# Convolution taps and softmax sums moved from VectorE to GpSimd, SSD decays moved out of attention

## The chip, the cores and the metric

The kernel runs on one core of a Trainium2 chip. The metric is device time in microseconds for one execution. Five engines work from queues of their own, each strictly in order: TensorE (PE), VectorE (DVE), ScalarE (ACT), GpSimd (POOL) and SyncE (SP), which here issues every DMA.

## The reference

Two layers of a hybrid block over 1024 latent tokens and 256 context tokens, model width 1024, all in float32:

```python
h = modulate(x, norm_g[i], shift, scale); h_c = modulate(ctx, ...)
z, xbc, dtr, q, k, v, ga, ua, ub, gc = split_cols(h @ w_in[i])
# SSD: 5-tap convolution, 12 heads of 64, state 128, chunks of 128, both directions
lmat = exp(where(mask, cum[t] - cum[s], -inf))          # the decays
y_diag = einsum('clsg,clsgr,csgrp->clgrp', C @ B.T, lmat, x * dt)
# attention: 12 heads, 4 key heads, 1280 keys (latents and context)
attn = softmax(q @ k.T) @ v * silu(ga)
# conformer: 31-tap depthwise convolution over 512 channels
u = silu(layernorm(dwconv(ua * sigmoid(ub), cm_conv_w) + cm_conv_b))
conv = (u @ pw_w + pw_b) * silu(gc)
x = x + gate * (concat([ssd, attn, conv]) @ w_out[i])
```

After the second layer a last rmsnorm gives the output. In layer 1 the context's rows are needed as keys and as the SSD's initial state alone, so there the conformer runs over 1024 columns and not 1295.

## The kernel before, in words

A product in float32 is made of three products of rounded halves (hi x hi, hi x lo, lo x hi; `mm3`). Weights are split as they arrive: ScalarE rounds the upper half (`wth`), GpSimd subtracts (`wtl`, L359).

Each layer goes through these stages:

1. Norms, then keys, values and queries in token-major form (`phase_b`).
2. Seventeen blocks of feature-major products (`block(i)`, `FM_UNITS`). Blocks 0 to 8 alternate between pairs of SSD channels (`xbc`) and a pair `ub`, `ua` of the conformer. Blocks 9 to 11 are the gate z, 12 and 13 gc, 14 to 16 ga. A gate goes through tanh on ScalarE and one VectorE instruction to DRAM (`gate`).
3. While these run, the convolutions run on VectorE. `conv_x(j)` is a tensor_scalar, four scalar_tensor_tensor (`xcv`), a tanh and one more, over 1282 columns; PE then transposes the result (`t<-msk,xcv`, `x<-msk,xcv`) and ScalarE copies it to `xsg`, from where it goes to DRAM. `conv_cm(j)`, j from 0 to 3, is one tensor_scalar and 30 scalar_tensor_tensor into the accumulator `cac[j]`. Its input `up` has two buffers, so the third `ua` is written when the first one's 31 taps are done. The tile `th` has one buffer, shared by `conv_x`'s tanh and the gate `ub`.
4. `cm_tail`, with all four `cac` complete: for each tile of 128 tokens PE transposes `cac` (`t<-msk,cac`), VectorE normalises, PE transposes back, silu, the split `uh`, `ul`; for each group of four tiles the pointwise product, times the gate gc. It runs beside blocks 9 to 16.
5. Attention (`attn`) with the SSD (`ssd`) beside it. A unit is two heads by 256 queries: 24 units against 1280 keys a layer, and 6 more of the context in layer 0. `maxima(i)` finds row maxima two units ahead (`a_sm`). `scores(i)` makes ten key tiles of scores and exponentials; these land in pairs, `a_p`, of which there are five buffers. The softmax sums are adds of pairs into `a_ac`, then one add of its halves, `a_a` (L981). `NG = [0, 1]` alternates from unit to unit: all on VectorE, or one add on GpSimd and three on VectorE (an add of two partial sums included). `values(i)` multiplies with v, `finish` sums `a_a` over keys by a product with `twos`, takes the reciprocal, multiplies, gates.
6. The SSD per chunk: `s_cb`, a broadcast load of the cumulated sums; GpSimd subtracts (L788), ScalarE does relu and exp, GpSimd multiplies with the masked B C product `s_cm` (L791); the tile `s_e` is then an operand of PE. Four such tiles a chunk, ten chunks in layer 0, eight in layer 1. Other products of the chunk (`s_wx`, `s_tm`, `s_xd`, `s_yo`) are GpSimd's as well.
7. The output product in two halves (`out_half`).

The order of the work isn't written by hand. `at(us)` gives the following instructions a due time, and when the kernel is built a planner plays the program through with costs of its own and takes, for each engine, the ready instruction with the earliest due time. The order that comes out is fixed; at run time an engine waits for whatever stands first in its queue. A tile pool that opens in the place of a closed one waits for the last user of the closed one's memory.

Of the kernel before, what the change touches and what calls it, by code (L numbers as in the profile page):

```python
# [9 lines left out]
F32R = mybir.dt.float32r  # L10
# [10 lines left out]
CM_PACE = 1.7  # L21
TAIL = 40.0
SSD_PACE = 25.0
# [4 lines left out]
FLAG = 7  # L28
NG = [0, 1]
A2B = 1  # L30
# [8 lines left out]
NT = T // 128  # L39
# [121 lines left out]
def build(tc, a, out, depth=DEPTH, dump=None):  # L161
# [272 lines left out]
    def phase_b(l, nh, b0, pp):  # L434
# [114 lines left out]
        def conv_cm(j, t0, pace):  # L549
            u, o = ups[j], cac[j]  # L550
            at(t0)
            ts(V, o[:, 0:NCM], u[:, 0:NCM], cw[:, j, 0:1], ALU.mult, cc(l, "cmb", j), ALU.add)
            for k in range(1, 31):
                at(t0 + k * pace)
                stt(o[:, 0:NCM], u[:, k:k + NCM], cw[:, j, k:k + 1], o[:, 0:NCM], ALU.mult, ALU.add)

        def conv_x(j, t0):
# [16 lines left out]
            if j < 8:  # L574
                at(t0 + XLAG)
                sg = mk(gp, [128, NT, 128], "xsg")
                for ta in (0, 4, 8):
                    n = min(4, NT - ta)
                    ps = mk(*((pt, [128, 4, 128], "t") if ta == 4 else (px, [128, 4, 128], "x")))
                    for t in range(ta, ta + n):  # L580
                        c0 = t * 128 + (2 if t >= 8 else 0)
                        tr(ps[:, t - ta, :], o[:, c0:c0 + 128], idf)
                    act(sg[:, ta:ta + n, :], ps[:, 0:n, :], AF.Copy)
                if j < 6:
                    d = xt_d[:, :, 128 * j:128 * j + 128]
                else:
                    d = bt_d[:, :, 128 * (j - 6):128 * (j - 6) + 128]
                Y.dma_start(out=d.rearrange("t p f -> p t f"), in_=sg)

# [63 lines left out]
        for i in range(9, 14):  # L653
            block(i)

        def cm_tail(c0):
            at(c0 - 10)
            pwh, pwl = wblock(tlp, wt, a["pww"][l], "pw", 1)
            hc = mk(tlp, [128, 16], "hc")
            ts(V, hc[:, 0:8], colc[l][:, CO["lng"][0]:CO["lng"][0] + 8], 0.5, ALU.mult)  # L660
            groups = [(0, 4), (4, 4)] + ([] if last else [(8, 2)])
            for tb, tn in groups:
                uh = mk(tlp, [128, 4, 512], "uh", F32R)
                ul = mk(tlp, [128, 4, 512], "ul", F32R)
                for t in range(tb, tb + tn):
                    at(c0 + 4 * t)
                    c1 = t * 128 + (15 if t >= 8 else 0)
# [20 lines left out]
                    act(uh[:, :, o:o + 128], v2, AF.Copy)  # L688
                    G.tensor_tensor(ul[:, :, o:o + 128], v2, uh[:, :, o:o + 128].bitcast(F32), ALU.subtract)
# [20 lines left out]
    def ssd(l, sp, c0, sv):  # L710
# [44 lines left out]
        for c in [8, 9] + list(range(8)):  # L755
# [3 lines left out]
            if c < 8 or not last:  # L759
                bT = mk(sp, [128, 2, 128], "s_bT", bufs=2)  # L760
                cT = mk(sp, [128, 2, 128], "s_cT", bufs=2)
                tk = slice(128 * c, 128 * c + 128)
                Y.dma_start(out=bT, in_=bT_d[:, :, tk].rearrange("g p t -> p g t"))
# [3 lines left out]
                ps = mk(px, [128, 512], "x")  # L767
                for g in range(2):
                    mm(ps[:, 128 * g:128 * g + 128], bT[:, g, :], cT[:, g, :], True, True)
                cm = mk(sp, [128, 2, 2, 128], "s_cm", bufs=1)  # L770
                for d, m in enumerate((um, lm)):
                    V.tensor_tensor(cm[:, d], ps[:, 0:256].rearrange("p (g t) -> p g t", g=2),
                                    m.unsqueeze(1).to_broadcast([128, 2, 128]), ALU.mult)
                xd = []
# [5 lines left out]
                for g in range(2):  # L780
                    for d in range(2):
                        h0 = 12 * d + 6 * g
                        cb = mk(sp, [128, 6, 128], "s_cb", bufs=2)
                        src = cum_d[24 * c + h0:24 * c + h0 + 6, :].rearrange("h t -> (h t)")
                        Y.dma_start(out=cb.rearrange("p h t -> p (h t)"),
                                    in_=src.unsqueeze(0).to_broadcast([128, 768]))
                        e = mk(sp, [128, 6, 128], "s_e", bufs=4)
                        G.tensor_tensor(e, cb, bc(cum[:, c, h0:h0 + 6], 6, 128), ALU.subtract)  # L788
                        act(e, e, AF.Relu, scale=-1.0)
                        act(e, e, AF.Exp, scale=-1.0)  # L790
                        G.tensor_tensor(e, e, cm[:, d, g].unsqueeze(1).to_broadcast([128, 6, 128]), ALU.mult)  # L791
                        E[d, g] = e
# [416 lines left out]
```

## Time and profile before

| | |
|---|---|
| median of 3 runs | 2921.86 us (2919.12 to 2928.43) |
| profiled execution | 2926.13 us, span 2924.1 us |
| PE / DVE / ACT / POOL busy | 93% / 74% / 36% / 40% of the span |
| feature blocks, with taps: layer 0, layer 1 | 299.6 to 603.2, 1804.4 to 2068.6 us |
| feature blocks, rest: layer 0, layer 1 | 603.2 to 797, 2068.6 to 2218 us |
| attention with SSD: layer 0, layer 1 | 797 to 1375, 2218 to 2712 us |
| mean granted TensorE clock | 0.965 |

The busy time of an engine counts from an instruction's start to its end, and what an instruction waits for after its start is inside it. PE's busy time is that of pipelined products with modelled ends. A mean over a line mixes instructions that ran alone with others that were held up; the view by tile gives minimum, median and maximum.

### The profile page before, as it was taken

Reading aid. Unit: us, or ns where it says so; the run is one execution under the profiler, and the core shown is the slowest. Engines: PE = TensorE matmul, PEld = TensorE weight load, DVE = VectorE, ACT = ScalarE, POOL = GpSimd, SP = SyncE. Lnnn points to the kernel's source line nnn. Section 1 sums busy time; section 2 is a strip of 40 time slices with the busy share of each in tenths; the row PEclk is TensorE's granted clock in tenths of the full one; section 3 lists DMA queues with packets and bytes.
Section 4 is the critical chain, followed back from the end, with each engine's and each line's share of the span. In section 5 each row is a group of like instructions: output and inputs, shape, how many; then the busy total and the mean of one; then the engine's idle time right before and its main releaser. Section 6 shows DMA issues by size and latency. Waiting matters only on the chain. (4 is left out here: it accounts for less than half of the span.)

```text
span 2924.1 us, 41057 instructions
## 1 busy us (share of the span) xinstructions
PE 2714.5 (93%) x15708; PEld 2111.4 (72%) x15708; DVE 2175.7 (74%) x2987; ACT 1062.2 (36%) x1801; POOL 1165.6 (40%) x832
## 2 busy tenths in 40 slices
PE   5999998999998888999999999999998998999998
PEld 3888876888856655666787998877886665666676
DVE  4476899973299989797445587999835989898644
ACT  4212221222245454454335222222224454644432
POOL 2244122232168677571112352222323667675111
PEclk9999998999999989899999999999999999999999
DMA  6551111223343222224645322113234232312554
GB/s 237 191 159 66 56 55 65 90 98 105 115 137 108 73 88 84 74 68 130 205 147 162 114 76 67 55 63 107 102 127 151 73 98 72 103 59 62 164 152 143
DMA packets 284035, 314.44 MB, mean 108 GB/s; under 512 B 27606, under 2 KB 219190, under 8 KB 282814
## 3 DMA queue, kind: packets, MB, share of 16 engines
q1 hardware_dynamic: 283838, 311.82, 33.5%
q8 instruction: 123, 2.02, 0.3%
q14 instruction: 74, 0.61, 0.1%
HBM read 236.25 MB, written 75.50 MB: 107 GB/s over the span
## 5 line engine op out<-in xcount | busy, mean ns | idle before, releaser
L193 PE MATMUL m<-hh,wth 128*128 128x512 f32 (+1 forms) x1440 | 533.7, 371 | 0.1
L193 PE MATMUL m<-hl,wth 128*128 128x512 f32 (+1 forms) x1440 | 532.2, 370 | 0.0
L193 PE MATMUL m<-hh,wtl 128*128 128x512 f32 (+1 forms) x1440 | 531.6, 369 | 0.0
L199 ACT ACTIVATE a_p<-m 128x512 f32<-128x512 f32 x492 | 285.5, 596 | 373.1 <-PE m L193 362.7
L208 DVE SCALAR_TENSOR_TENSOR cac<-up,cmw,cac 128x1295 f32<-128x1295 f32 (+1 forms) x240 | 383.2, 1617 | 1.9
L935 DVE TENSOR_REDUCE a_sm<-m 128x1 f32<-128x512 f32 (+1 forms) x600 | 331.0, 583 | 52.8 <-PE m L193 50.2
L359 POOL TENSOR_TENSOR wtl<-wr,wth 128x1024 fp32r<-128x1024 f32 x68 | 201.9, 2969 | 404.2 <-ACT wth L199 404.1
L193 PEld LDWEIGHTS m<-hh,wth 128*128 128x128 f32 x1440 | 273.0, 190 | 47.8 <-ACT th L199 0.5
L193 PEld LDWEIGHTS m<-hh,wtl 128*128 128x128 f32 x1440 | 272.5, 189 | 48.1
L193 PEld LDWEIGHTS m<-hl,wth 128*128 128x128 f32 x1440 | 272.7, 189 | 47.3
L193 PE MATMUL m<-q_a,k_a 128*128 128x512 f32 (+1 forms) x656 | 255.3, 399 | 23.1 <-ACT a_p L199 10.9
L193 PE MATMUL m<-k_a,q_a 128*128 128x512 f32 (+1 forms) x600 | 242.0, 440 | 24.9 <-DVE a_sm L935 19.3
L193 PE MATMUL t<-a_p,vs 128*64 128x256 f32 x1968 | 250.9, 397 | 0.9 <-ACT a_p L199 0.4
L193 PE MATMUL m<-woh,yl 128*128 128x512 f32 x576 | 227.7, 397 | 6.1 <-DVE yl L1101 5.9
L193 PE MATMUL m<-woh,yh 128*128 128x512 f32 x576 | 226.6, 396 | 5.2 <-ACT yh L199 5.2
L193 PE MATMUL m<-wol,yh 128*128 128x512 f32 x576 | 226.6, 395 | 0.8 <-DVE wol L1077 0.8
L193 PE MATMUL m<-q_b,k_b 65*128 65x512 f32 (+1 forms) x656 | 223.1, 350 | 0.0
L193 PEld LDWEIGHTS t<-a_p,vs 128*64 128x64 f32 x1968 | 138.7, 142 | 89.1 <-issue 17.2
L193 PEld LDWEIGHTS m<-q_a,k_a 128*128 128x128 f32 x656 | 129.3, 197 | 84.3 <-ACT a_p L199 23.4
L193 PEld LDWEIGHTS m<-k_a,q_a 128*128 128x128 f32 x600 | 117.0, 201 | 99.6 <-DVE a_sm L935 38.2
L199 ACT ACTIVATE wth<-wr 128x1024 fp32r<-128x1024 f32 (+1 forms) x84 | 89.3, 1063 | 255.6 <-DMA wr<-in_wfm 136.2
L193 PE MATMUL m<-wth,hh 128*128 128x256 f32 (+1 forms) x608 | 173.6, 288 | 1.3 <-ACT wth L199 0.8
(239 smaller groups left out, 5629.5 us busy)
## 6 DMA issues: line engine op xcount, KB each, us to landing
wr<-in_wfm SPq DMA_DIRECT2D x68, 512.0 KB, 3.6
s_cb<-cum_d SPq DMA_DIRECT2D x72, 384.0 KB, 3.7
ada_w<-in_adaw SPq DMA_DIRECT2D x32, 512.0 KB, 4.6
wor<-in_wout SPq DMA_DIRECT2D x64, 256.0 KB, 3.1
s_x<-xt_d SPq DMA_DIRECT2D x38, 384.0 KB, 3.2
yf<-ys_d SPq DMA_DIRECT2D x36, 384.0 KB, 3.9
yf<-ya_d SPq DMA_DIRECT2D x36, 384.0 KB, 4.2
yf<-yc_d SPq DMA_DIRECT2D x36, 256.0 KB, 2.9
```

The lines of the kernel that those rows point to most:

```text
L193: P.matmul(o, l, r, start=start, stop=stop)
L199: S.activation(o, i, f, **k)
L208: V.scalar_tensor_tensor(o, i, s, i1, op0, op1)
L359: (e or G).tensor_tensor(lo[:, s], raw, hi[:, s].bitcast(F32), ALU.subtract)
L935: V.tensor_reduce(sm[:, 2 * x + t, j:j + 1], ps[:, 0:kn], axis=AX.X, op=ALU.max)
```

## The change

Three things at once, with the due times that go with them.

- 45 taps a layer leave VectorE: all of `conv_cm(0)` (its first one becomes a ScalarE instruction, 30 become a scaling on ScalarE into `cmt`, of which there are two buffers, and an add on GpSimd) and the last 15 of `conv_cm(2)`.
- The decays are made in a new function `decays`, a chunk in turn with a tile of the conformer tail, and go through DRAM (`e_d`). Their multiplication moves from GpSimd to VectorE. The SSD only loads the finished tiles.
- `NG = [4]`: all four adds of pairs of each unit against 1280 keys are GpSimd's; VectorE keeps `a_a`.

The conformer tail goes in pairs of tiles, due 17 us apart (4 us before), from `TAIL = 20` (40 before). Blocks 9 to 16 get a lead of 100 us in the due times of their weights and of their gates. `xsg` becomes three smaller tiles with a store each.

```diff
-TAIL = 40.0
+TAIL = 20.0
+GTAPS = {0: 30, 2: 15}
-NG = [0, 1]
+NG = [4]
...
         def conv_cm(j, t0, pace):
             u, o = ups[j], cac[j]
             at(t0)
-            ts(V, o[:, 0:NCM], u[:, 0:NCM], cw[:, j, 0:1], ALU.mult, cc(l, "cmb", j), ALU.add)
-            for k in range(1, 31):
+            nv = 31 - GTAPS.get(j, 0)
+            if nv > 1:
+                ts(V, o[:, 0:NCM], u[:, 0:NCM], cw[:, j, 0:1], ALU.mult, cc(l, "cmb", j), ALU.add)
+            else:
+                act(o[:, 0:NCM], u[:, 0:NCM], AF.Identity, scale=cw[:, j, 0:1], bias=cc(l, "cmb", j))
+            for k in range(1, nv):
                 at(t0 + k * pace)
                 stt(o[:, 0:NCM], u[:, k:k + NCM], cw[:, j, k:k + 1], o[:, 0:NCM], ALU.mult, ALU.add)
+            for k in range(nv, 31):
+                at(t0 + (nv - 1) * pace + (k - nv) * 2 * pace)
+                m = mk(up_p, [128, 1295], "cmt", bufs=2)
+                act(m[:, 0:NCM], u[:, k:k + NCM], AF.Copy, scale=cw[:, j, k:k + 1])
+                G.tensor_tensor(o[:, 0:NCM], o[:, 0:NCM], m[:, 0:NCM], ALU.add)
...
         def block(i):
-            at(u0 - 20)
+            lead = 100 if i >= 9 else 0
+            at(u0 - 20 - lead)
...
+                    at(tt - lead)
                     fm_fin(ps, n, j, t0, tn)
...
+        def decays(c, t0):
+            cum = sv[1]
+            at(t0)
+            bT = mk(ep, [128, 2, 128], "e_b")
+            cT = mk(ep, [128, 2, 128], "e_c")
...
+            at(t0 + 8)
+            ps = mk(px, [128, 512], "x")
+            for g in range(2):
+                mm(ps[:, 128 * g:128 * g + 128], bT[:, g, :], cT[:, g, :], True, True)
+            cm = mk(ep, [128, 2, 2, 128], "e_m")
...
+                    at(t0 + 8 + 4 * (2 * d + g))
+                    e = mk(ep, [128, 6, 128], "e_e", bufs=3)
+                    src = cum_d[24 * c + h0:24 * c + h0 + 6, :].rearrange("h t -> (h t)")
+                    Y.dma_start(out=e.rearrange("p h t -> p (h t)"), in_=src.unsqueeze(0).to_broadcast([128, 768]))
+                    G.tensor_tensor(e, e, bc(cum[:, c, h0:h0 + 6], 6, 128), ALU.subtract)
+                    act(e, e, AF.Relu, scale=-1.0)
+                    act(e, e, AF.Exp, scale=-1.0)
+                    V.tensor_tensor(e, e, cm[:, d, g].unsqueeze(1).to_broadcast([128, 6, 128]), ALU.mult)
+                    Y.dma_start(out=e_d[c][2 * d + g], in_=e.rearrange("p h t -> p (h t)"))
...
-            groups = [(0, 4), (4, 4)] + ([] if last else [(8, 2)])
+            groups = [(b, 2) for b in range(0, 8 if last else NT, 2)]
...
-                    at(c0 + 4 * t)
+                    at(c0 + 17 * t)
...
-        cm_tail(g0 + TAIL)
+        order = list(range(8)) if last else [8, 9] + list(range(8))
+        for t in cm_tail(g0 + TAIL):
+            decays(order[t], g0 + TAIL + 17 * t)
...
                 for g in range(2):
                     for d in range(2):
-                        h0 = 12 * d + 6 * g
-                        cb = mk(sp, [128, 6, 128], "s_cb", bufs=2)
...
                         e = mk(sp, [128, 6, 128], "s_e", bufs=4)
-                        G.tensor_tensor(e, cb, bc(cum[:, c, h0:h0 + 6], 6, 128), ALU.subtract)
-                        act(e, e, AF.Relu, scale=-1.0)
-                        act(e, e, AF.Exp, scale=-1.0)
-                        G.tensor_tensor(e, e, cm[:, d, g].unsqueeze(1).to_broadcast([128, 6, 128]), ALU.mult)
+                        Y.dma_start(out=e.rearrange("p h t -> p (h t)"), in_=e_d[c][2 * d + g])
                         E[d, g] = e
```

More of the change, by code (lines that the diff above doesn't have):

```diff
@@ L260, in build @@
     cum_d = dr([NT * 24, 128], "cum_d")
+    e_d = [dr([4, 128, 768], f"e_d{c}") for c in range(NT)]
     gz_d = dr([6, 128, T], "gz_d")
@@ L575, in conv_x @@
                 at(t0 + XLAG)
-                sg = mk(gp, [128, NT, 128], "xsg")
+                if j < 6:
+                    d = xt_d[:, :, 128 * j:128 * j + 128]
+                else:
+                    d = bt_d[:, :, 128 * (j - 6):128 * (j - 6) + 128]
                 for ta in (0, 4, 8):
@@ L582, in conv_x @@
                         tr(ps[:, t - ta, :], o[:, c0:c0 + 128], idf)
[L583 to L588, printed above, removed]
+                    sg = mk(gp, [128, 512], "g_o", bufs=2)[:, 0:128 * n].rearrange("p (t f) -> p t f", t=n)
+                    act(sg, ps[:, 0:n, :], AF.Copy)
+                    Y.dma_start(out=d[ta:ta + n].rearrange("t p f -> p t f"), in_=sg)
         def gate(ps, t0, n, d):
@@ L654, in phase_b, with bc @@
             block(i)
+        def bc(x, n, w):
+            return x.unsqueeze(2).to_broadcast([128, n, w])
+        def decays(c, t0):
+            cum = sv[1]
+            tk = slice(128 * c, 128 * c + 128)
+            at(t0)
+            bT = mk(ep, [128, 2, 128], "e_b")
+            cT = mk(ep, [128, 2, 128], "e_c")
+            Y.dma_start(out=bT, in_=bT_d[:, :, tk].rearrange("g p t -> p g t"))
+            Y.dma_start(out=cT, in_=cT_d[:, :, tk].rearrange("g p t -> p g t"))
+            at(t0 + 8)
[3 more added lines that the diff above has]
+            cm = mk(ep, [128, 2, 2, 128], "e_m")
+            for d, m in enumerate((um, lm)):
+                V.tensor_tensor(cm[:, d], ps[:, 0:256].rearrange("p (g t) -> p g t", g=2),
+                                m.unsqueeze(1).to_broadcast([128, 2, 128]), ALU.mult)
+            for d in range(2):
+                for g in range(2):
+                    h0 = 12 * d + 6 * g
+                    at(t0 + 8 + 4 * (2 * d + g))
[7 more added lines that the diff above has]
+                    Y.dma_start(out=e_d[c][2 * d + g], in_=e.rearrange("p h t -> p (h t)"))
+        ep = pool(s3, f"ep{l}")
         def cm_tail(c0):
@@ L660, in cm_tail @@
             ts(V, hc[:, 0:8], colc[l][:, CO["lng"][0]:CO["lng"][0] + 8], 0.5, ALU.mult)
-            groups = [(0, 4), (4, 4)] + ([] if last else [(8, 2)])
+            groups = [(b, 2) for b in range(0, 8 if last else NT, 2)]
             for tb, tn in groups:
-                uh = mk(tlp, [128, 4, 512], "uh", F32R)
-                ul = mk(tlp, [128, 4, 512], "ul", F32R)
+                uh = mk(tlp, [128, 4, 256], "uh", F32R)
+                ul = mk(tlp, [128, 4, 256], "ul", F32R)
                 for t in range(tb, tb + tn):
-                    at(c0 + 4 * t)
+                    at(c0 + 17 * t)
                     c1 = t * 128 + (15 if t >= 8 else 0)
@@ L674, in cm_tail @@
                     rs_pow(bs[:, 9:10], bs[:, 7:8], 1.0, bs[:, 8:9], 1)
-                    xn = mk(gp, [128, 512], "xn", bufs=1)
+                    xn = mk(tlp, [128, 512], "xn", bufs=1)
                     ts(V, xn, ps.rearrange("p j t -> p (j t)"), bs[:, 6:7], ALU.subtract, bs[:, 9:10], ALU.mult)
@@ L689, in cm_tail @@
                     G.tensor_tensor(ul[:, :, o:o + 128], v2, uh[:, :, o:o + 128].bitcast(F32), ALU.subtract)
+                    yield t
                 n = tn * 128
-                at(c0 + 4 * (tb + tn))
+                at(c0 + 17 * (tb + tn))
                 for f in range(4):
-                    gcs = mk(gp, [128, 512], "gcs")
+                    gcs = mk(tlp, [128, 256], "gcs", bufs=2)
                     Y.dma_start(out=gcs[:, 0:n], in_=gc_d[f][:, tb * 128:tb * 128 + n])
@@ L759, in ssd @@
             if c < 8 or not last:
-                bT = mk(sp, [128, 2, 128], "s_bT", bufs=2)
                 cT = mk(sp, [128, 2, 128], "s_cT", bufs=2)
                 tk = slice(128 * c, 128 * c + 128)
-                Y.dma_start(out=bT, in_=bT_d[:, :, tk].rearrange("g p t -> p g t"))
                 Y.dma_start(out=cT, in_=cT_d[:, :, tk].rearrange("g p t -> p g t"))
@@ L766, in ssd @@
                 Y.dma_start(out=gz, in_=gz_d[:, :, tk].rearrange("g p t -> p g t"))
[L767 to L773, printed above, removed]
                 xd = []
```

3 lines of the change are left out of this document (removed).

## The prediction

> **What bounds the kernel now.** I read the page's slices first, then the table by stage, cut at the first and the last convolution tap of each layer.
>
> ```profile
> DVE  4476899973299989797445587999835989898644
> POOL 2244122232168677571112352222323667675111
> GB/s 237 191 159 66 56 55 65 90 98 105 115 137 108 73 88 84 74 68 130 205 147 162 114 76 67 55 63 107 102 127 151 73 98 72 103 59 62 164 152 143
> ```
> ```profile
> 299.60:603.20 303.60, 278.85 (x1422) 235.24 (x1420) 298.51 (x194) 62.03 (x95) 69.33 (x43) 0.96 0.21 68
> 603.20:797.00 193.80, 193.28 (x1038) 164.90 (x1038) 75.39 (x155) 45.86 (x74) 44.96 (x31) 1.00 0.31 106
> 797.00:1375.00 578.00, 514.96 (x3369) 348.00 (x3370) 504.59 (x707) 295.48 (x509) 370.42 (x222) 0.93 0.31 94
> 1804.40:2068.60 264.20, 251.22 (x1194) 207.07 (x1192) 263.20 (x187) 61.60 (x91) 64.06 (x42) 0.98 0.24 77
> 2068.60:2218.00 149.40, 149.09 (x674) 121.27 (x674) 63.36 (x115) 35.66 (x53) 38.57 (x26) 1.00 0.35 116
> 2218.00:2712.00 494.00, 447.89 (x2922) 302.57 (x2922) 435.04 (x619) 253.42 (x436) 313.18 (x187) 0.95 0.30 90
> ```
>
> The busy columns are PE, PEld, DVE, ACT, POOL; then clock, DMA share, GB/s. Rows 1 and 4 are the taps: DVE is busy 298.5 of 303.6 us and 263.2 of 264.2, POOL a quarter of it. Rows 2 and 5, the rest of the feature products with the conformer tail, are PE alone, never idle. Rows 3 and 6 are attention with the SSD: PE near 90%, DVE 88%, POOL 64%. By these shares POOL is free to relieve DVE. The next rows say why that fails.
>
> ```profile
> 349.71 1.56 DVE L208 SCALAR_TENSOR_TENSOR cac<-up,cmw,cac 128x1295 f32<-128x1295 f32 x1
> 364.71 2.40 POOL L359 TENSOR_TENSOR wtl<-wr,wth 128x1024 fp32r<-128x1024 f32 x1 [14.63 <-ACT wth L199]
> 364.88 3.60 DVE L208 SCALAR_TENSOR_TENSOR cac<-up,cmw,cac 128x1295 f32<-128x1295 f32 x1
> ```
>
> A tap takes 1.56 us alone. The one that starts 0.17 us into a POOL subtraction takes 3.60: it waits until 367.11, when POOL ends, and runs its whole length after that (367.11 + 1.4 = 368.5). A DVE instruction that reads two SBUF operands and a POOL tensor_tensor do not overlap; they take turns. So I keep a ledger: uncontended times of the two kinds, added up, for 299.6 to 603.2.
>
> ```profile
> L208 DVE SCALAR_TENSOR_TENSOR cac<-up,cmw,cac 128x1295 f32<-128x1295 f32 x120 | 209.6, 1765 | 1.0
> L208 DVE SCALAR_TENSOR_TENSOR xcv<-xpad,scw,xcv 128x1282 f32<-128x1282 f32 x32 | 53.1, 1658 | 0.0
> L205 DVE TENSOR_SCALAR xcv<-xpad,scw 128x1282 f32<-128x1282 f32 x8 | 16.0, 1997 | 0.0
> L208 DVE SCALAR_TENSOR_TENSOR xcv<-th,xcv 128x1282 f32<-128x1282 f32 x8 | 11.9, 1485 | 0.0
> L359 POOL TENSOR_TENSOR wtl<-wr,wth 128x1024 fp32r<-128x1024 f32 x19 | 68.0, 3580 | 179.1 <-ACT wth L199 179.1
> ```
> ```profile
> 509.18 0.94 DVE L205 TENSOR_SCALAR cac<-up,cmw,colc 128x1295 f32<-128x1295 f32 x1
> 1979.74 1.27 DVE L208 SCALAR_TENSOR_TENSOR cac<-up,cmw,cac 128x1024 f32<-128x1024 f32 x1
> 1980.94 0.80 DVE L205 TENSOR_SCALAR cac<-up,cmw,colc 128x1024 f32<-128x1024 f32 x1
> ```
>
> Layer 0: 120 x 1.56 + 32 x 1.55 + 12 x 0.94 + 8 x 1.49 + 19 x 2.40 = 305 us in a stretch of 303.6. Layer 1, with taps of 1.27: 152 + 50 + 11 + 12 + 20 x 2.40 = 273 in 264. The taps' stretch is bound by the taking of turns, at 100%, and not by DVE.
>
> How PE pays for it:
>
> ```profile
> PE x L196 <- DVE xcv L208: 12.8, 2, 10.6
> PE x L196 <- ACT xsg L199: 5.4, 2, 5.0
> PE t L196 <- DVE xcv L208: 4.2, 1, 4.2
> PE t L196 <- DVE xcv L208: 11.7, 3, 6.1
> ```
> ```profile
> 505.32 0.42 DVE L208 SCALAR_TENSOR_TENSOR up<-th,m 128x256 f32<-128x256 f32 x1
> 603.23 0.44 PE L196 MATMUL t<-msk,cac 128*128 128x128 f32 x2 [2.44 <-DVE cac L208]
> 1979.15 0.68 DVE L208 SCALAR_TENSOR_TENSOR up<-th,m 128x512 f32<-128x512 f32 x1
> 2068.68 0.44 PE L196 MATMUL t<-msk,cac 128*128 128x128 f32 x2 [1.26 <-DVE cac L208]
> ```
>
> The first three rows are layer 0's, the fourth layer 1's (total us, times, longest). PE's queue has one order, laid down in advance; transposes of the convolved tiles stand between feature products, and PE waits for them: 24.8 us in layer 0 (12.8 + 5.4 + 4.2 + 2.4), 13.0 in layer 1. DVE's own excess is 298.5 minus its uncontended 273 (260 for two operands, 13 for 22 PSUM ones of 0.42 to 0.68), about 25. I conclude that the order was planned as if the two engines did not hinder each other.
>
> **The change, part by part.**
>
> *45 taps a layer.* Each leaves DVE (1.56 us, layer 1 1.27) and becomes a scaling on ScalarE and an add on POOL. Its price in turns is bounded by the plain adds:
>
> ```profile
> L974 POOL TENSOR_TENSOR a_ac<-a_p,a_p x24: 2358/2373/3350, 844.8 to 2720.8; 128x1024 f32<-128x1024 f32 x24
> L689 POOL TENSOR_TENSOR ul<-lv,uh x18: 1282/1294/1337, 617.1 to 2156.9; 128x512 fp32r<-128x512 f32 x18
> L199 ACT ACTIVATE th<-xcv x20: 1262/1276/1285, 267.3 to 2036.3; 128x1282 f32<-128x1282 f32 x20
> ```
>
> (2.37 - 1.29)/512 = 2.11 ns a column, so 2.37 + 271 x 2.11 ns = 2.94 us for 1295 columns; 2.37 for layer 1's 1024. The ledger grows by 45 x (2.94 - 1.56) = 62 us in layer 0 and 45 x (2.37 - 1.27) = 49 in layer 1. Bounds: minus 70 and minus 57 if POOL's adds cost DVE nothing (the 3.60 row excludes most of that), plus 62 and 49 if all collide. Since the ledger is full, I take the upper ends. ScalarE's 46 instructions of 1.28 us (59 us a layer) fit: it is busy 62 of 303.6. POOL in order has the weight splits (wtl) between the adds; PE stands a block of weights ahead, so I cost that at nothing; if the lead is lost, each block waits for one or two adds, 3 to 9 us.
>
> The Trainium skill, "SBUF — State Buffer", section "Who interferes with whom", states the mechanism as a rule: a VectorE instruction with two SBUF inputs and a GpSimd one that reads SBUF share a port pair under an exclusive lock held for the whole instruction. The 3.60 us row agrees with it. By the rule the taps cost 62 and 49 us; by the busy shares alone they would save 70 and 57. "GPSIMD Engine Reference" of the Trainium skill, "Performance versus the Vector engine", gives 4497 ns for an add of 2048 columns, in proportion 2.84 us for 1295: by it the sum would be 58 instead of 62.
>
> So the last tap of layer 0 ends near 603 + 62, less two or three weight splits that PE's wait holds back (6): 660. In layer 1: 2069 + 49 - 5 = 2113.
>
> *Where PE meets it.* In the planned order DVE has fewer taps, so the tail's first transposes stand earlier. After the last gated piece (505.7 us, less the 22.4 that PE had waited by then: 483) DVE has block 3's 31 taps (47.7), two SSD convolutions (17.2) and a few gates (3.5): 551 on a clock without waits, where before it was 603.2 - 24.8 = 578. The new due time (TAIL 20, then 17 us a tile) is earlier still, so it doesn't hold them back. PE arrives early and waits until 660: 109 us lost in place of 24.8, a loss of 84. Part of it falls sooner: the third `up` buffer is the first one again, free only when block 0's 30 adds are done (88 us of adds with 8 to 10 splits and DVE's turns after 300, so 445 to 475, where PE wants it at 411). The ledger's end is the same. Layer 1: 1979.8 - 11.7 + 39 + 17.2 + 2.7 = 2027, waits until 2113: 86 in place of 13.0, a loss of 73.
>
> *Decays.* Per chunk 4 subtractions, 8 activations, 4 multiplications (now on DVE), 2 mask products, 2 products, and 10 DMAs (bT and cT, 4 loads, 4 stores) go beside blocks 10 to 16; in the SSD 4 loads stay, of the finished tiles.
>
> ```profile
> L788 POOL TENSOR_TENSOR s_e<-s_cb,d_cum x72: 1462/1472/2537, 810.0 to 2648.3; 128x768 f32<-128x768 f32 x72
> L791 POOL TENSOR_TENSOR s_e<-s_e,s_cm x72: 1806/1856/2824, 878.2 to 2665.6; 128x768 f32<-128x768 f32 x72
> L199 ACT ACTIVATE s_e<-s_e x144: 827/843/851, 811.5 to 2650.7; 128x768 f32<-128x768 f32 x144
> L974 DVE TENSOR_TENSOR a_ac<-a_p,a_p x48: 1160/1222/2902, 832.0 to 2724.6; 128x1024 f32<-128x1024 f32 x48
> ```
>
> Ten chunks: POOL 40 x 1.47 = 59 us, ScalarE 80 x 0.84 = 67, DVE 40 x about 0.92 (in proportion to 1.22) and masks, 45. The stretch after the taps has POOL 45, ScalarE 46, DVE 75 of 194: it holds them. Their 31 MB (15.7 in, 15.7 out) add about 140 GB/s over 222 us to 106; the first slice shows 237 moved. SP issues in order, so weights stand behind a store that waits for DVE's multiplication; covered by the block of lead. I cost all this at nothing; without that cover, some 5 us a block, 40 a layer. The transposed tiles' three stores in place of one, and the tail in pairs of tiles, likewise nothing.
>
> *Attention.*
>
> ```profile
> PE t L193 <- DVE a_a L981: 28.2, 17, 5.9
> PE m L193 <- DVE a_sm L935: 12.5, 14, 2.4
> PE m L193 <- DVE a_sm L935: 17.4, 22, 2.2
> PE t L193 <- DVE a_a L981: 7.7, 11, 1.2
> ```
>
> (The first two are layer 0.) DVE loses 3.5 adds of 1.22 us in each of 24 units, 102 us a layer, and the turns lost to them. POOL gains 84 adds x 2.37 = 199 and loses 40 x (1.47 + 1.86) = 133: about 66 more, on 370 busy that shrink with DVE's turns; it stays under 80%. PE's wait for the maxima (29.9 in both) should mostly go: 24. Its wait for a_a (35.9) I leave: four POOL adds in a row, among the SSD's, replace DVE's chain; `a_a`, the two `twos` products and then the reciprocal stand behind them. Other small waits give 5. The clock, 0.93 and 0.95, comes back a little, 15. Together 45 us. Bounds: plus 10 (a_a's wait doubled), and minus 130: idle PE is 63 + 46, and the clock lost at most 41 + 25, part of it in the same moments.
>
> **Sum**, on the profiled run (span 2924.1, 2926.13 with what lies around it): 2926 + 84 + 73 - 45 = 3038. The median shown is 2921.86, 4.3 lower: 3035.
>
> **Rivals.**
>
> *Faster.* The collision is milder than the ledger says: POOL adds while DVE serves PSUM, as gates and maxima do. Then the 24.8 + 13.0 us of waits go, and attention gives 45 to 100: 2922 - 38 - 45 = 2840, down to 2785. For it: DVE is the busiest engine in rows 1 and 4. Against it: only 13 us of DVE's work there is from PSUM, and the ledger fills 100%. It decides if a POOL add costs DVE less than the 1.56 us it saves. Chance 0.17.
>
> *No change.* The tail's transposes stand far enough behind feature products that PE doesn't meet the late taps; only the `up` buffer's wait remains (about 20 us in layer 0, 15 in layer 1), against attention's 45: 2912, between 2895 and 2940. For it: PE has 222 us of products left after 551. Against: at 603.23 and 2068.68 PE already waits for the last tap before, so the transposes stand right where it was expected. Chance 0.13.
>
> *Worse.* Behind late adds on POOL stand weight splits, and behind waiting stores on SP stand weights; the lead of a block is lost and PE waits twice: 3035 + 60 = 3095 or more. Chance 0.1.
>
> **Numbers.** The forecast has 0.6, with its own range 2965 to 3080 (attention 0 to 100, the tail's place 20 us either way). The range for all leaves out the faster case below 2900 and the far end of the worse: 2900 to 3095. Within 0.3% of 2922 (about what a measurement tells from no change) lie 2913 to 2931: part of the no-change case, 0.05; its faster part joins the faster rival: 0.23; slower 0.72.
>
> **What would show it.** Right: DVE's taps of 4.4 us beside POOL's; last tap near 660 and 2113; PE idle for tens of us before t<-msk,cac or an `up` evacuation; attention some 20 us shorter in each layer with DVE near 60%. Wrong: last tap at or before 603; PE still full from 300 to 800; or a wait for a_a that grows past 60 us.

## The result, and the profile after

| | before | after |
|---|---|---|
| median of 4 runs, us | 2923.14 (2919.12 to 2928.43) | 3091.13 (3086.11 to 3093.18) |
| ratio, 95% interval | | 1.0571 (1.0549 to 1.0593) |
| span of the profiled execution, mean clock | 2924.1, 0.965 | 3089.9, 0.939 |

The changed kernel is 5.7% slower: 168 us, where the prediction said 113 (3035 us, range 2900 to 3095). The slices of the whole span:

```profile
DVE  4476699983546767685445575999845576767444
POOL 3253974844437787765112355938344488885511
GB/s 226 186 154 61 51 29 70 42 147 177 250 226 139 112 101 104 87 89 54 191 145 165 99 79 64 45 45 62 160 203 228 195 78 98 104 87 94 90 154 145
```

The sixth to eighth digits of DVE still stand at 9, as before, where POOL now has 7, 4 and 8 and had 2: the taps' stretch is full of both. The last row shows what came new: in slices 10 to 12, beside layer 0's conformer tail, 177 to 250 GB/s where the kernel before moved 105 to 137. The table by stage is cut at the same marks as before, with one more row a layer: from the last feature product to attention's first scores, which I call the passage.

```profile
307.30:661.50 354.20, 265.40 (x1328) 223.26 (x1326) 314.65 (x144) 122.51 (x142) 246.98 (x90) 0.87 0.18 58
661.50:906.20 244.70, 225.68 (x1234) 192.54 (x1235) 123.94 (x225) 99.17 (x141) 106.12 (x69) 0.96 0.63 209
906.20:946.30 40.10, 22.06 (x71) 10.57 (x69) 14.29 (x23) 11.37 (x20) 16.55 (x12) 0.62 0.77 249
946.30:1470.90 524.60, 498.56 (x3331) 338.73 (x3331) 365.73 (x603) 236.43 (x429) 381.62 (x218) 0.95 0.30 93
1903.80:2201.00 297.20, 239.02 (x1101) 195.31 (x1099) 269.85 (x137) 105.71 (x131) 197.21 (x85) 0.91 0.20 66
2201.00:2393.00 192.00, 177.44 (x838) 145.65 (x839) 103.44 (x164) 80.67 (x109) 91.64 (x58) 0.95 0.63 208
2393.00:2447.40 54.40, 30.14 (x101) 17.28 (x99) 19.14 (x33) 16.08 (x26) 21.81 (x16) 0.63 0.71 233
2447.40:2910.20 462.80, 445.30 (x2981) 300.98 (x2981) 326.35 (x531) 215.95 (x390) 360.05 (x198) 0.98 0.29 89
```

The columns are those of the prediction's table; rows 3 and 7 are the passages. The kernel before had these:

```profile
796.00:803.30 7.30, 3.01 (x23) 2.00 (x21) 1.47 (x4) 4.04 (x10) 0.24 (x1) 0.81 0.57 173
2217.00:2227.00 10.00, 4.90 (x29) 3.19 (x28) 2.11 (x4) 5.83 (x12) 2.38 (x2) 0.67 0.68 204
```

Against the kernel before, at the same marks: taps +50.6 and +33.0 us; rest of the feature products +51.9 and +43.6 (192.8 and 148.4 before); passages +32.8 and +44.4 (7.3 and 10.0 before); attention -53.4 and -49.2 (578.0 and 512.0 before); between attention and the next layer's taps +9.8, before the first tap +7.7, after the last unit -5.4. These add up to 165.8, the difference of the two spans.

In the taps' stretch the taking of turns is plain. VectorE's instructions of the changed kernel, and then GpSimd's of the same microseconds:

```profile
436.99 4.20 DVE L209 SCALAR_TENSOR_TENSOR xcv<-th,xcv 128x1282 f32<-128x1282 f32 x1
441.11 3.65 DVE L209 SCALAR_TENSOR_TENSOR cac<-up,cmw,cac 128x1295 f32<-128x1295 f32 x1
444.69 4.20 DVE L209 SCALAR_TENSOR_TENSOR xcv<-xpad,scw,xcv 128x1282 f32<-128x1282 f32 x1
```
```profile
439.80 3.60 POOL L361 TENSOR_TENSOR wtl<-wr,wth 128x1024 fp32r<-128x1024 f32 x1
443.37 4.17 POOL L566 TENSOR_TENSOR cac<-cac,cmt 128x1295 f32<-128x1295 f32 x1
```

The weight split starts at 439.80, gets its turn when VectorE ends at 441.1, and runs 2.4 us to 443.4; the tap that started at 441.11 runs its 1.5 us after that, to 444.8; the add that started at 443.37 then runs 2.9 us, to 447.5. Whoever starts while the other is at work waits it out, and the wait counts as busy. The whole of it in layer 0, by tile:

```profile
L209 DVE SCALAR_TENSOR_TENSOR cac<-up,cmw,cac x75: 1552/1564/4294, 380.7 to 660.0; 128x1295 f32<-128x1295 f32 x75
L566 POOL TENSOR_TENSOR cac<-cac,cmt x45: 2925/4122/6737, 310.1 to 621.2; 128x1295 f32<-128x1295 f32 x45
```

(Minimum, median, maximum in ns.) An add takes 2.93 us alone. More than half of the taps that VectorE kept ran unhindered (median 1.56 us); it is mostly the adds that waited (median 4.12 us). The ledger of the stretch is 75 x 1.56 + 32 x 1.55 + 11 x 0.94 + 8 x 1.49 on VectorE and 45 x 2.93 + 18 x 2.40 on GpSimd: 364 us, in 354.2 (VectorE's instructions overlap each other by 0.07 to 0.08 us in the rows above, some 10 us over 126 of them). PE's waits there, layer 0 and then the largest of layer 1:

```profile
PE m L194 <- DVE g_o L209: 24.9, 2, 20.2
PE t L197 <- DVE xcv L209: 20.4, 2, 20.0
PE x L197 <- DVE xcv L209: 15.4, 1, 15.4
PE m L194 <- ACT th L200: 10.7, 1, 10.7
PE x L197 <- ACT g_o L200: 10.4, 1, 10.4
PE t L197 <- DVE cac L209: 7.2, 1, 7.2
```
```profile
PE t L197 <- DVE xcv L209: 25.8, 2, 22.6
PE m L194 <- ACT xpad L200: 9.7, 2, 7.7
PE t L197 <- DVE cac L209: 9.0, 1, 9.0
```

Layer 0's add up to 89 us, as does 354.2 minus 265.4; before it was 24.8. They lie at whatever PE's fixed order has next of VectorE's: a gate (`g_o`), a convolved SSD tile (`xcv`), the staged transposes. The last tap itself is waited for 7.2 and 9.0 us.

Attention's rows show VectorE at 70% and PE busier at a clock of 0.95 and 0.98. PE's waits for the sums (`a_a`) in layer 0, and its largest of layer 1, for the maxima (`a_sm`):

```profile
PE t L194 <- DVE a_a L1014: 6.1, 5, 2.1
```
```profile
PE m L194 <- DVE a_sm L968: 7.3, 13, 1.4
```

They were 28.2 us for `a_a` in layer 0 and 17.4 for `a_sm` in layer 1.

### The profile page after: what moved, and what is told of

Its sections match the earlier page's. It is cut to its first block, busy times and chain, and to the rows that moved or that the text cites. A ratio compares the mean times of both kernels' runs of the same rounds, so it can differ in the third digit from the quotient of the medians.

```text
span 3089.9 us, 42323 instructions
## 1 busy us (share of the span) xinstructions
PE 2756.9 (89%) x15900; PEld 2140.4 (69%) x15900; DVE 2042.7 (66%) x2831; ACT 1174.8 (38%) x1893; POOL 1680.6 (54%) x1018
## 5 line engine op out<-in xcount | busy, mean ns | idle before, releaser
L194 PE MATMUL m<-hh,wth 128*128 128x512 f32 (+1 forms) x1440 | 547.5, 380 | 50.1 <-DVE g_o L209 25.4
L194 PE MATMUL m<-hh,wtl 128*128 128x512 f32 (+1 forms) x1440 | 544.8, 378 | 0.0
L194 PE MATMUL m<-hl,wth 128*128 128x512 f32 (+1 forms) x1440 | 543.6, 377 | 0.0
L1007 POOL TENSOR_TENSOR a_ac<-a_ac,a_p 128x1024 f32<-128x1024 f32 x144 | 344.2, 2390 | 38.5 <-ACT a_p L200 34.9
L209 DVE SCALAR_TENSOR_TENSOR cac<-up,cmw,cac 128x1295 f32<-128x1295 f32 (+1 forms) x150 | 354.5, 2371 | 2.0
L566 POOL TENSOR_TENSOR cac<-cac,cmt 128x1295 f32<-128x1295 f32 (+1 forms) x90 | 315.5, 3506 | 20.7 <-ACT cmt L200 11.9
L194 PEld LDWEIGHTS m<-hl,wth 128*128 128x128 f32 x1440 | 280.9, 195 | 47.9
L194 PE MATMUL m<-q_a,k_a 128*128 128x512 f32 (+1 forms) x656 | 246.5, 387 | 12.6 <-ACT a_p L200 8.7
L194 PE MATMUL m<-k_a,q_a 128*128 128x512 f32 (+1 forms) x600 | 229.9, 424 | 14.7 <-DVE a_sm L968 8.9
L696 POOL TENSOR_TENSOR e_e<-e_e,d_cum 128x768 f32<-128x768 f32 x72 | 115.4, 1608 | 173.8 <-DMA e_e<-cum_d 137.5
## 6 DMA issues: line engine op xcount, KB each, us to landing
wr<-in_wfm SPq DMA_DIRECT2D x68, 512.0 KB, 3.9
ada_w<-in_adaw SPq DMA_DIRECT2D x32, 512.0 KB, 3.9
```

What stands on the lines that cost most here:

```text
L194: P.matmul(o, l, r, start=start, stop=stop)
L209: V.scalar_tensor_tensor(o, i, s, i1, op0, op1)
L566: G.tensor_tensor(o[:, 0:NCM], o[:, 0:NCM], m[:, 0:NCM], ALU.add)
L696: G.tensor_tensor(e, e, bc(cum[:, c, h0:h0 + 6], 6, 128), ALU.subtract)
L1007: e.tensor_tensor(o, prev[-1], pt2, ALU.add)
```

## The experiments

Stretches in us, layer 0 / layer 1: the taps; the last tap to attention's first scores; attention to its last sum. "Change" is the ratio less one, on 2922 us. The stretches are those of one traced execution; f2's was its fastest, 2951 us, where the other three took 2968 to 2972.

| kernel | median | ratio (95%) | change | taps | tap to scores | attention |
|---|---|---|---|---|---|---|
| before | 2921 to 2930 | | | 304 / 264 | 200 / 158 | 578 / 512 |
| after | 3091 | 1.0571 (1.0549 to 1.0593) | +167 | 354 / 297 | 285 / 246 | 525 / 463 |
| e1 no taps | 2963 | 1.0125 (1.0089 to 1.0161) | +37 | 307 / 264 | 264 / 219 | 522 / 464 |
| e2 taps only | 3062 | 1.0462 (1.0433 to 1.0492) | +135 | 350 / 298 | 223 / 181 | 575 / 507 |
| e3 sums only | 2987 | 1.0205 (1.0165 to 1.0244) | +60 | 305 / 262 | 203 / 158 | 584 / 553 |
| e4 decays only | 2982 | 1.0190 (1.0161 to 1.0218) | +56 | 306 / 264 | 263 / 215 | 531 / 469 |
| f2 due 10 us apart | 2968 | 1.0133 (1.0100 to 1.0167) | +39 | 308 / 264 | 256 / 216 | 522 / 464 |
| f3 small loads | 2933 | 1.0019 (1.0007 to 1.0032) | +6 | 306 / 265 | 246 / 203 | 524 / 468 |
| f4 half of the decays | 2995 | 1.0236 (1.0211 to 1.0262) | +69 | 306 / 264 | 250 / 200 | 553 / 489 |
| f5 22 taps | 3037 | 1.0374 (1.0354 to 1.0394) | +109 | 330 / 281 | 280 / 237 | 521 / 464 |
| g1 two PSUM tiles | 3020 | 1.0341 (1.0317 to 1.0365) | +100 | 306 / 266 | 296 / 227 | 539 / 471 |
| g2 g1 and f2 | 3017 | 1.0322 (1.0292 to 1.0352) | +94 | 307 / 264 | 290 / 229 | 532 / 474 |
| h1 change, two PSUM tiles | 3153 | 1.0793 (1.0767 to 1.0818) | +232 | 353 / 298 | 315 / 248 | 542 / 474 |
| i1 schedule only | 2991 | 1.0211 (1.0189 to 1.0233) | +62 | 305 / 262 | 224 / 186 | 583 / 512 |

### The parts one by one

e1, the change without its taps:

```diff
-GTAPS = {0: 30, 2: 15}
+GTAPS = {}
```

> The changed kernel with all convolution taps back on VectorE; decays beside the tail and the sums on GpSimd stay. Theory of turns (VectorE's two-operand instructions and GpSimd's exclude each other, so 45 taps moved cost 62 and 49 us a layer more than they save): the last taps end at about 303 and 264 us after the first again (354 and 297 with the change), the decays start some 50 us earlier and no longer hold up attention, attention keeps its gain of 103; 2923 + 16 (the small shifts ahead of the blocks) - 103 + 0 to 30 = 2835 to 2870. Rival, theory of places (it is the due times, the staging of the transposed tiles and the decays' loads and stores that make PE wait, not the taps): the blocks stay 150 to 180 us longer than before, 3000 or more.

e2, the kernel before with the taps' code of `conv_cm` and the smaller staging tiles (`xn` and `gcs` in another pool, for room):

```diff
+GTAPS = {0: 30, 2: 15}
...
+            for k in range(nv, 31):
+                m = mk(up_p, [128, 1295], "cmt", bufs=2)
+                act(m[:, 0:NCM], u[:, k:k + NCM], AF.Copy, scale=cw[:, j, k:k + 1])
+                G.tensor_tensor(o[:, 0:NCM], o[:, 0:NCM], m[:, 0:NCM], ALU.add)
...
-                sg = mk(gp, [128, NT, 128], "xsg")
+                    sg = mk(gp, [128, 512], "g_o", bufs=2)[:, 0:128 * n].rearrange("p (t f) -> p t f", t=n)
```

> The kernel before with the 45 taps a layer on ScalarE and GpSimd, and the smaller staging tiles that make room for them; decays, sums and due times as before. Theory of turns: last taps 350 to 365 and 295 to 310 us after the first; the blocks lose 84 + 73 us and nothing is won elsewhere: 2923 + 157 = 3080 (3040 to 3100). Theory of places: within 20 us of before, 2905 to 2945.

e3, the kernel before with the sums on GpSimd:

```diff
-NG = [0, 1]
+NG = [4]
```

> The kernel before with all pair sums on GpSimd alone (NG = [4]); decays stay in the SSD. In turns, attention's ledger in layer 0 goes from 465 of 578 us (326 GpSimd, 139 VectorE) by +199 - 102 to 562 of 578: full. If the gain of attention comes from relieving the ledger, this part alone gains nothing: 2900 to 2960, with GpSimd over 85% busy in attention. If it comes from relieving VectorE, whose busy share falls all the same, it keeps most of the 103: 2820 to 2860.

e4, the change without taps and without sums:

```diff
-GTAPS = {0: 30, 2: 15}
+GTAPS = {}
-NG = [4]
+NG = [0, 1]
```

> The changed kernel with the taps back on VectorE and with the sums shared as before (NG = [0, 1]); only the decays' move and the due times stay. The ledger of attention in layer 0 falls by 131 to 334 of 578, VectorE keeps 102 us of adds but loses fewer turns. Turns: about half of the gain, 2923 + 16 - 50 + 0 to 30 = 2870 to 2920. If VectorE's own adds are what holds attention: no gain, 2920 to 2955.

The taps are settled from both sides. Alone they cost 135 us; taken out of the change they give back 130 (1.0571 against 1.0125). Without them the stretches are again as before, layer 0 and 1 of e1:

```profile
308.80:616.20 307.40, 279.80 (x1423) 235.90 (x1421) 301.26 (x194) 66.66 (x101) 76.64 (x46) 0.95 0.22 70
1835.50:2099.70 264.20, 251.26 (x1194) 207.21 (x1192) 262.03 (x187) 65.85 (x97) 77.06 (x45) 0.98 0.26 82
```

The other forecasts missed. e1 came at 2963 and e4 at 2982, so the change is a loss even without taps. Alone, the sums make attention 6 us longer in layer 0 and 41 in layer 1 (e3's attention in both, and PE's largest wait in layer 0):

```profile
808.20:1392.30 584.10, 509.26 (x3360) 345.89 (x3360) 393.74 (x621) 290.45 (x501) 527.11 (x306) 0.92 0.30 91
2245.80:2798.80 553.00, 483.38 (x3034) 322.74 (x3032) 373.97 (x557) 262.16 (x454) 479.13 (x272) 0.90 0.28 85
```
```profile
PE m L193 <- ACT a_p L199: 23.0, 12, 7.9
```

GpSimd is busy 90% and 87% of it: scores wait for exponentials (23.0 us in layer 0, 5.3 before; 18.3 in layer 1, 6.6 before), and these wait for GpSimd's adds to free one of the five `a_p` buffers (58.7 and 67.6 us of ScalarE's waits; 2.8 and none before). With the decays gone from attention the same edit gains a little: e4 to e1 is 9.4 and 5.1 us in attention, 1.0190 to 1.0125 in all, with intervals that just touch, so this small gain is not sure.

### Half of the taps

f5, the change with 22 taps in place of 45:

```diff
-GTAPS = {0: 30, 2: 15}
+GTAPS = {0: 15, 2: 7}
```

> The changed kernel with 22 instead of 45 taps a layer on GpSimd (15 of block 0, 7 of block 2). Ledger of turns: VectorE 256 - 22 x 1.56 = 222, GpSimd 49 + 22 x 2.93 = 113, 335 us for layer 0's taps, 325 to 335 measured (307 with none, 354 with 45); layer 1 221 - 28 + 51 + 52 = 296 by sum, 283 to 287 by the 1.03 seen; time midway between 2963 and 3091: 3010 to 3040. Rival: what costs is the chain of 30 adds that the third up buffer waits for; with 15 it is off the path, and the time falls to 2960 to 2980 with the taps' stretch at most 315.

The stretch grows in step with the taps: 307, 330, 354 in layer 0 and 264, 281, 297 in layer 1, for 0, 22 and 45. Neither half nor all of them are taken for nothing, and the rival, the chain of 30 adds that the third `up` buffer waits for, had asked for at most 315 in layer 0.

### What the rest of the change costs

In e1 the last tap is at its old place, yet attention starts 64 and 60 us later than it should by the old distance: 31 and 24 in the feature products, and 32 and 36 in the passage, in which PE has little to do. Three edits of e1 and e4 went after it. f2 makes tail and decays due earlier:

```diff
-                    at(c0 + 17 * t)
+                    at(c0 + 10 * t)
...
-            decays(order[t], g0 + TAIL + 17 * t)
+            decays(order[t], g0 + TAIL + 10 * t)
```

> No taps on GpSimd (as e1_no_taps, 2963), and the tail's tiles with their decays due 10 us apart instead of 17. In e1 the blocks still take 31 and 24 us more after the last tap than before, and 40 and 46 us pass between the last block and the first scores (7 and 10 before). Theory of lateness: attention's first tiles lie in memory that the last decays give free, and these end with the blocks because they are due that late; due earlier, the passage falls to 10 to 20 us in each layer: 2890 to 2920. Theory of transfers: decays load and store 31 MB in layer 0 beside 223 GB/s, and closer together they delay weights and gates: no gain, 2950 to 2990.

f3 loads one head's row for six, a sixth of the broadcast; it leaves out the sums of the other five heads and is there for the price of the loads alone:

```diff
-                    Y.dma_start(out=e.rearrange("p h t -> p (h t)"), in_=src.unsqueeze(0).to_broadcast([128, 768]))
-                    G.tensor_tensor(e, e, bc(cum[:, c, h0:h0 + 6], 6, 128), ALU.subtract)
+                    e1 = mk(ep, [128, 128], "e_1", bufs=3)
+                    Y.dma_start(out=e1, in_=src.unsqueeze(0).to_broadcast([128, 128]))
+                    G.tensor_tensor(e, e1.unsqueeze(1).to_broadcast([128, 6, 128]), bc(cum[:, c, h0:h0 + 6], 6, 128), ALU.subtract)
```

> As e1_no_taps, but each decay tile loads one head's row (64 KB broadcast) and uses it for six heads, instead of six rows (384 KB); so it leaves out five of six heads' cumulated sums. Stores and all compute instructions stay. Theory of transfers: 13 of 31 MB less, the blocks' tail stretch shrinks by 10 to 20 us a layer, and the passage too: 2880 to 2920. Theory of lateness: the end of the decays is set by due times, only some 2 us of load latency go: 2945 to 2965.

f4 is e4 with the decays of chunks 8, 9, 0, 1, 2 (layer 1: 0 to 3) early, and those of the others in the SSD as before:

```diff
+EARLY = [(8, 9, 0, 1, 2), (0, 1, 2, 3)]
...
+            if order[t] in EARLY[l]:
-            decays(order[t], g0 + TAIL + 17 * t)
+                decays(order[t], g0 + TAIL + 17 * t)
```

> As e4_decays_only (2982; no taps, sums shared as before), but only five of ten chunks' decays in layer 0 and four of eight in layer 1 beside the tail, the rest inside the SSD as in the kernel before. If the cost of the early decays is their late end (passage 40 and 46 us), it goes wholly, as these end in the middle of the tail: passage back to 10, tail stretch half its loss (13 and 12 us), half of attention's gain of 90 kept: 2925 + 16 - 45 + 28 + 5 = 2930 (2910 to 2945). If the cost is by the amount moved, half of it: 2925 + 16 - 45 + 62 = 2958.

f2 changed nothing that can be measured (1.0133 against 1.0125), and its last decay was stored 217 us after layer 0's last tap, where e1's was stored after 225: it is not the due times that make the decays late. f3 gave 18 and 15 us of the stretch from last tap to scores: the loads are a part of it. f4, at 2995 us above both of its forecasts, ended its last early decay in layer 0 at 741 us and still had a passage of 37: the decays' lateness is not what holds attention's start. What does is seen at SP, in attention's first load (`vs`); before and e4 in both layers, and the change in layer 0:

```profile
L846 SPq DMA_DIRECT2D vs<-v_d x2: 371/371/371, 762.5 to 2186.7; - x2
```
```profile
L879 SPq DMA_DIRECT2D vs<-v_d x2: 371/508/646, 850.6 to 2295.3; - x2
```
```profile
L879 SPq DMA_DIRECT2D vs<-v_d x1: 360/360/360, 918.5 to 918.5; - x1
```

In each it goes out within 8 us of the start of the conformer tail's last pointwise product (762.2 and 2186.3 before; 843.5 and 2288.8 in e4; 912.0 in the change); in the change's layer 1 the load stands behind loads of the SSD on SP's queue and goes out at 2425.2, 11 us after that product. In the kernel before, SP's wait in front of the load ends with the product. The first scores follow 22 to 41 us later. In the kernel before, 34 and 30 us of feature products were left at that moment and covered this; in the change there are none. The tail now goes in pairs: in layer 0 20 passes through one PSUM tile (`v`), where there were 12, in turn with feature products. My next theory was that the single tile made it late, and that a second one would mend it. g1 (from e1), g2 (from f2) and h1 (from the whole change) take it from the ring that the feature products use:

```diff
-                    ps = mk(pv_, [128, 512], "v")
+                    ps = mk(pv_, [128, 512], "v") if f % 2 == 0 else mk(pm, [128, 512], "m")
```

> The change without its taps (45 taps back on TensorE), with the pointwise products of the odd output blocks accumulated in the ring of PSUM tiles that the taps use, instead of all of them in the single pointwise tile. Theory P (attention's first loads wait for the end of the conformer tail, and the tail is late because its passes go one after the other through one PSUM tile, and pairs of tiles make 20 and 16 passes of what were fewer): the passages from the last feature product to the first scores fall from 40 and 46 us to 8 to 15, and the median from 2963 to 2895 to 2910. Rival (transfers of the decays and the memory of their pool make the passage): passages stay near 40 and 46, and the median stays within 10 us of 2963.

(The taps are back on VectorE in g1, not on TensorE, and the ring is that of the feature products.)

> As g1, and the tail and the decays due 10 us apart instead of 17. Theory P: as g1 or a little less, 2880 to 2900 us, passages 8 to 15 us. Rival: 2960 to 2975 us, passages near 40 and 46.

> The whole change, with the same edit of the pointwise products as g1. Theory P: passages fall from 40 and 54 us to about 10, and the median from 3091 to 3015 to 3035. Rival: 3080 to 3100 us.

All three missed: they are slower by 55 to 65 us than what they came from. The passages did fall, to 7 to 10 us, but only because the feature products now end after the tail. g1 from the last tap to the last feature product, and its passage; then PE's largest waits from 610 to 960 us, and the load:

```profile
613.60:900.00 286.40, 217.64 (x1169) 187.61 (x1170) 132.87 (x229) 104.10 (x146) 105.28 (x68) 0.85 0.56 186
900.00:909.60 9.60, 3.99 (x25) 2.62 (x24) 1.48 (x4) 4.49 (x10) 2.28 (x2) 0.70 0.71 215
```
```profile
PE x L197 <- DVE e_m L687: 25.3, 3, 14.3
PE x L194 <- DVE lv L206: 20.1, 6, 7.7
```
```profile
L879 SPq DMA_DIRECT2D vs<-v_d x2: 371/371/371, 885.7 to 2330.1; - x2
```

The tail's last product started at 882.7, later than e1's 845.6, with the load at 885.7. In the order planned with this edit PE waits 45 us for the PSUM tile `x`, until VectorE has read the products for the decays' masks (`e_m`) or the input of the tail's next step (`lv`) out of it, and is busy 218 of 286. g2 shows the other side: there the tail ended 201 us after layer 0's last tap (f2: 223), but the feature products ended only after 280. So a second PSUM tile can bring the tail forward, and in these planned orders it costs more than that; why the orders got worse was not followed further.

i1 leaves of the change only what goes with its parts: pairs of tiles due 17 us apart, `TAIL = 20`, the lead of 100 us, the smaller staging tiles. Against f4:

```diff
-EARLY = [(8, 9, 0, 1, 2), (0, 1, 2, 3)]
+EARLY = [(), ()]
```

> No taps, no sums, no decays moved: of the change only what goes with them stays, the conformer tail in pairs of tiles due 17 us apart from TAIL 20, the lead of 100 us for blocks 9 to 16, and the smaller staging tiles. With e4 (all decays early) and f4 (half of them) it makes a row of three. From the last tap to the first scores e4 takes 263 and 215 us, f4 250 and 200, the kernel before 200 and 158. Theory S (it is the tail in pairs, with its passes through one pointwise tile, that makes the stretch long): 235 to 245 and 190 us here, attention as before (578 and 512), so 2985 to 3005 us. Theory D (it is the decays' work, stood between the feature products, that makes it): about 205 and 162 us here, and the median 2925 to 2945. f4 lies nearer to e4 than to before, which speaks for S.

```profile
613.50:807.70 194.20, 194.16 (x1125) 170.07 (x1125) 74.67 (x166) 40.56 (x65) 44.95 (x31) 0.99 0.28 95
807.70:837.70 30.00, 13.09 (x39) 6.46 (x38) 6.72 (x12) 12.18 (x21) 14.19 (x10) 0.56 0.88 270
2113.50:2259.40 145.90, 145.90 (x742) 122.54 (x742) 62.22 (x123) 32.84 (x49) 40.99 (x27) 1.00 0.31 104
2259.40:2299.70 40.30, 23.31 (x71) 11.11 (x69) 11.63 (x20) 15.65 (x26) 22.13 (x15) 0.62 0.82 258
```
```profile
L903 SPq DMA_DIRECT2D vs<-v_d x2: 362/366/371, 809.0 to 2269.0; - x2
```

The time is theory S's. With no decay moved and no tap, the kernel takes 62 us more than before; layer 0's stretch of 224 us lies between the two forecasts, layer 1's 186 near S's. Its feature products are undisturbed (PE full, 194.2 and 145.9 us), and the passages are already 30 and 40 us: the load goes out 1.3 and 9.6 us after the last feature product, where before it went out 34 and 30 ahead of it. The passages hold 53 of the 66 us between the two profiled executions (the largest of the rest: +9 before the first tap, +8 between the layers, +5 in layer 0's attention, -6 after the last unit). What e4 adds in the stretch, 39 and 29 us, is the decays (theory D): 30 and 24 in the feature products, 9 and 5 in the passage.

i1's trace also shows where its tail loses the time. The tail's first rounding (`uh`, the input of the pointwise product) comes 13 to 14 us after the last tap in both layers of i1 and of the kernel before; from there to the last pointwise product the tail takes 178 and 136 us, where it took 146 and 104. Each next group's `uh` starts 0.1 us after the last pointwise product of the group before it has ended (in i1 at 682.1, 716.4, 745.7 and 775.1, and so in all three cases of the kernel before): the groups go strictly one after the other, and pairs make five and four of them out of three and two. A second PSUM tile doesn't touch that. Whether the due times of 17 us, the lead or the staging tiles have a share in the 178 and 136 isn't shown: no run changes the pairs alone.

In attention the decays' leaving is the gain. i1's two rows and e4's, and PE's wait for `a_a` in layer 0 in i1 and in e4:

```profile
837.70:1420.60 582.90, 522.57 (x3372) 353.73 (x3372) 511.41 (x711) 295.43 (x506) 354.27 (x214) 0.92 0.29 87
2299.70:2811.50 511.80, 467.64 (x3017) 312.75 (x3017) 456.30 (x633) 257.36 (x446) 290.52 (x175) 0.95 0.27 81
877.40:1408.80 531.40, 497.57 (x3317) 335.02 (x3316) 452.67 (x683) 236.94 (x428) 191.91 (x133) 0.96 0.30 91
2321.90:2791.10 469.20, 446.65 (x2960) 300.44 (x2958) 411.24 (x612) 217.06 (x389) 170.04 (x112) 0.97 0.28 85
```
```profile
PE t L195 <- DVE a_a L1038: 20.1, 11, 3.9
```
```profile
PE t L194 <- DVE a_a L1014: 3.4, 5, 1.4
```

i1's attention is 582.9 and 511.8 us, e4's 531.4 and 469.2: 51.5 and 42.6 us less. What left the stage is 133 and 107 us of GpSimd's work, which took turns with VectorE's, and 58 and 40 us of ScalarE's; the two are not told apart. By the rows, 48 of the 94 us are idle time of PE, and 46 its busy time: 112 records of products fewer, and a clock of 0.96 and 0.97 in place of 0.92 and 0.95. But 39 and 29 come back between the last tap and attention, 3 in and ahead of the taps' stretches, 3 between the layers and 7 after the last unit: of 94 us the two profiled executions keep 13.

## Why the prediction was right or wrong

The change adds up as a ladder: schedule alone +62 us (i1), decays moved -6 more (e4; the intervals overlap, so not told from none), sums -19 (e1; the intervals touch), taps +130 (the change).

*Bound of the taps' stretch.* Right. The ledger of turns gave the price: an add takes 2.93 us and 2.35 (said: 2.94 and 2.37; 2.84 is the estimate from the page "GPSIMD Engine Reference" of the Trainium skill, section "Performance versus the Vector engine"), the last tap came at 661.5 (said: 660), and the stretch grew by 50.6 and 33.0 us (said: 57 and 44, from the old last tap). e1, e2 and f5 show it from three sides. The ledger is a good price, not an exact one: layer 1's makes 316 us, some 306 without the overlap of VectorE's own instructions, in 297.2, so about 10 us ran at once there. The sign that I named, taps of 4.4 us, came near for the longest alone (4.29). The rule of the Trainium skill that I set beside it ("SBUF — State Buffer", "Who interferes with whom") is borne out by the rows at 437 to 447 us. Layer 1's last tap came at 2201.0 where I said 2113, since everything ahead of it was later: 1903.8 for its first tap against 1804.4.

*Where PE meets it.* Right in kind, too large in size, wrong in place. I had PE lose 109 and 86 us before the tail's first transpose; it lost 89 and 58, and 7.2 and 9.0 of them there. The planned place of the transpose was not what counted: every gate and every convolved tile on VectorE's queue was late before it. The third `up` buffer was first written at 475.7, at the end of my 445 to 475. All taps cost 130 us in place of 157.

*POOL's weight splits and SP's queue.* Right that they don't decide: no wait of PE for a block's weights (`wth`, `wtl`) is among those above. SP did wait (its two largest waits of the change from 661 to 947 us):

```profile
SPq L695 <- DMA e_d<-e_e: 43.0, 26, 5.7
SPq L700 <- DVE e_e L699: 29.0, 26, 4.3
```

Loads of decays stood behind the freeing of `e_e`, and their stores behind VectorE, in an order in which everything else is issued too.

*Decays at nothing, and the tail in pairs "likewise nothing".* This is the step that failed. The decays cost 39 and 29 us between the last tap and attention. My reserve of 40 us a layer comes near that by luck: it was for weights that lose their lead, and in e4 PE waits there for VectorE's part of the tail instead (in layer 0 `gcs` 6.3, `cac` 5.1, `lv` 4.4, `bs` 2.8 us; no block's weights), and VectorE is busy 125 of the 225 us from the last tap to the last feature product, where i1 has 75 of 194. The pairs, with the due times that go with them, I passed over: 53 us in the passages, because I counted the tail's work on engines that had room, and not when its last product ends. What hid attention's start before was 34 and 30 us of feature products behind that last product; I did not ask for it, and the load at 762.5 against 796.0 would have shown it.

*Attention at -45.* Right in sign, the term mis-sized: -53 and -49, 102 in all, within the bound of 130. I gave the gain to the sums and left PE's wait for `a_a` in place. It is the other way round: 94 us come from the decays' leaving, 26 of them in that wait (20.1 to 3.4 us in layer 0, 9.8 to 0.7 in layer 1), and 14 from the sums; alone, the sums cost 60. VectorE's share fell to 70%, not near 60.

That the time lies in the range is partly luck, since the errors cancel: taps 27 us too dear, attention 57 too small a gain; the remainder of the miss of 56, some 140 us left out, is what e1 shows before attention (124) and before the first tap and between the layers (about 20). The time fell at the upper end of the range; the case called worse (3095 and more) had the time nearly right, for waits that are not among those above.

## What to carry to other kernels

Where two engines take turns, work moved between them must be priced by the sum of both, and the one that does the same work slower makes the sum larger however idle it looks. Work moved out of a busy stage is paid again in the stage it goes to unless that stage has slack at its own end: look for the load or the buffer that opens the next stage, who releases it, and how much is left on the bound engine at that moment. Test a change's schedule alone as well as its parts; here the rearrangement alone cost 62 us, more than all that the decays and the sums gave back.

## What was not expected of the hardware

- The exclusion can hold the other side for several instructions. In the change a weight split of 2.40 us took 11.78, from 504.62 on, while six instructions of VectorE's ran one after the other at 1.55 to 1.56 us each. Elsewhere the two alternate: eight taps on VectorE took 32.5 us (from 548.44), 4.1 each, in turn with the adds and a weight split:

```profile
504.62 11.78 POOL L361 TENSOR_TENSOR wtl<-wr,wth 128x1024 fp32r<-128x1024 f32 x1 [5.79 <-ACT wth L200]
548.44 32.48 DVE L209 SCALAR_TENSOR_TENSOR cac<-up,cmw,cac 128x1295 f32<-128x1295 f32 x8
```

- The granted clock falls in the stretches where PE waits: 0.96 to 0.87 in the taps' stretch, 0.56 to 0.63 in passages where PE is busy 44 to 58%. The Trainium skill, "TensorE: Matmul & The Clock Gate", section "What's actually happening", has a gate that halves the clock until PE has been busy for a while; the rows agree in direction. So PE's idle time may cost more than itself: part of the taps' 130 us, against 64 and 45 us more of idle time, may be that; it was not measured apart.
